# All five engines of the recurrence blocks 2 to 14 in one written order, with matmul banks read in place

## The chip, the cores and the metric

One core of one Trainium2 chip runs one launch of the kernel. The metric is the device time of that launch in microseconds (us). Differences are counted against the kernel before, whose three runs took 2610.59, 2611.43 and 2615.81 us (median 2611.43). Five engines work side by side, each through its own queue in order: TensorE (PE, matmuls), VectorE (DVE), ScalarE (ACT), GpSimd (POOL), and SyncE (SP), which here only issues DMAs.

## The reference, cut to what matters

One decoder layer over 2048 positions of width 1024. A normalised input goes through one large projection into two groups of heads, an SSD group and an RWKV7 group; both are mixed back, and a gated convolutional feed-forward follows. The part at issue is the RWKV7 group and the convolution that feeds the SSD group:

```python
p = p + (_token_shift(p) - p) * f32(mu)              # own column and the column one position before
r, w_lo, k, v, a_lo, g_lo = jnp.split(p, [i1, i2, i3, i4, i5], axis=-1)
...
def step(S, inp):                                    # the recurrence, one position after the other
    r_t, w_t, k_t, v_t, a_t, b_t = inp
    sa = jnp.einsum("bhij,bhj->bhi", S, a_t)
    S = S * w_t[:, :, None, :] + sa[..., None] * b_t[:, :, None, :] + v_t[..., None] * k_t[:, :, None, :]
    return S, jnp.einsum("bhij,bhj->bhi", S, r_t)
...
xbc = jax.nn.silu(_causal_dwconv(xbc, conv_w, conv_b))   # four taps: positions t-3 to t
```

All arithmetic is float32; the kernel computes its large products from float16 halves of weights and activations.

## The kernel before, in words

The first of three phases, `phase_R`, takes the sequence in 16 blocks of 128 positions. The weights stay in SBUF. For one block `it` it does, in the names of the code:

- `load`: reads 128 rows of x, normalises them, splits them into a high and a low float16 half, and turns both by a DMA transpose into `xt`. Three columns of the block before stand ahead of the 128, for the shift and the taps.
- `d`, groups 0 to 13: the projection, 24 matmuls of 128x129 each (line 301). Two groups share one PSUM bank of the tag `mm`, which has two buffers. After the second group ACT copies the bank to SBUF (`raw`, line 439) and writes the columns scaled by one minus mu (line 441); DVE adds the columns one position earlier, scaled by mu, out of `raw` (line 443). Groups 0 and 1 give `WA` and `GL`, then `tk`, `tr`, `tv` follow.
- `conv`, groups 0 to 7: the same with 131 columns and the same `mm` banks. ACT copies the bank (`rc`, line 455); POOL makes the first tap with the bias (line 464); DVE adds three taps for each of the two groups (line 469); ACT takes a tanh (line 473), DVE finishes the silu (line 474), SP stores.
- `low`, `scan`, `keys`, `norm`, `receptance`: decays, their running sums (`Pv`, a scan on DVE, line 508), their exponentials (`Pi` and `Pv`, ACT, lines 512 and 513), and the normalised keys. `norm` starts with the product `nq` and needs a logarithm and an exponential on ACT, each with a table load (lines 514 and 529).
- `gram`: the within-chunk products, masked by DVE into `G` (line 563). `solve` and `chain`: a triangular inverse, 31 pairs of small DVE operations (`tmp`, line 594, and `xl`, line 597), each of which needs the one before; its input goes out to HBM and back in another layout (`ATd`, `atl`), and so does its result (`XTd`, `XT`).
- `turn`, `merge`: DVE transposes a quarter of `XT` into `XW` (line 639), and two rounds of small products (`pw`, `po`) complete the inverse. `own`, `update`, `state`, twice, for the two chunks of 64 positions: the part of the recurrence that goes from chunk to chunk. `update` makes `pu`, which ACT copies to `UV` (line 696); `state` makes `pS` from it (line 713), and DVE adds it to the kept state `S`.
- `values`, `gate`, `finish`: the group norm, the bonus and the gate; the result is stored for the next phase.

The loop over blocks is a software pipeline. In iteration `it` the front part (`f`) works on block `it`, the back part (`b`) on block `it - 1`, the last piece (`a`) on block `it - 2`, and `n.load` prepares block `it + 1`. The table `PLAN`, a text of words such as `f.d.0 b.values`, gives the order in which iterations 2 to 14 call the functions. PE follows that order to the letter (its schedule is manual throughout). DVE and ACT follow the written order in iteration 0 alone; from iteration 1 on the tile framework's scheduler chooses, at build time, the order of DVE, ACT, POOL and SP. On the chip each engine then executes its fixed list, and an instruction that waits holds up all that stand behind it on its engine.

Within a function all instructions are issued at one place of `PLAN`. So the chain of block `it - 1` stands complete on DVE ahead of the scan of block `it`.

The later phases, the SSD group with the mixing (`phase_S`) and the feed-forward (`phase_F`), are not touched.

## Time and profile before

The profiled execution has a span of 2614.0 us from its first to its last instruction, with a mean granted PE clock of 0.975. That is 2.6 us over the median of the three runs and inside their range.

| stretch | length, us | PE busy | DVE busy | ACT busy | POOL busy | PE clock |
|---|---|---|---|---|---|---|
| whole program | 2614.0 | 2438.8 | 1968.8 | 1211.4 | 1310.1 | 0.975 |
| iterations 2 to 14, 145.0 to 865.5 us | 720.5 | 676.4 | 570.3 | 410.3 | 352.2 | 0.99 |
| one of the 13 iterations, mean | 55.42 | 52.03 | 43.87 | 31.56 | 27.10 | |

Iteration 2 begins near 145 us and iteration 15 near 865.5 us; both are read from the start of `f.d.0` on PE (the product `vt`, which `PLAN` puts behind the first three `d` groups, starts some 2.8 us later). Busy time of an engine is the union of its instructions. Matmuls overlap, so 24 matmuls of 222 ns each take 1.4 us together. In a row of the timeline the first number is the start, the second the length of the group, and the bracket gives the idle time of the engine ahead of it and the work that ended it.

### The profile page before, as it was taken

What the parts mean: (1) busy time and instruction counts of PE and PEld (TensorE: products, weight loads), DVE (VectorE), ACT (ScalarE), POOL (GpSimd) and SP (SyncE); (2) the same over time, 40 slices, a digit from 0 to 9 for tenths busy, and PEclk for the clock granted to TensorE, in tenths of its full rate; (3) what the DMA queues carried; (4) which work ended last, traced back from release to release, by engine and by line L of the source; (5) the groups of instructions that cost most, each with busy time, mean ns of one, the idle gap of its engine ahead of it and who ended that gap; (6) DMA issues with size and microseconds to landing.
All of it is one profiled execution on the core that took longest, in us unless ns stands there. A gap on an engine that the chain in (4) does not pass through costs nothing. (4 is left out here: it accounts for less than half of the span.)

```text
span 2614.0 us, 53918 instructions
## 1 busy us (share of the span) xinstructions
PE 2438.8 (93%) x21212; PEld 1535.9 (59%) x21212; DVE 1968.8 (75%) x3687; ACT 1211.4 (46%) x2467; POOL 1310.1 (50%) x1356
## 2 busy tenths in 40 slices
PE   5899999999999889999987999999989999999998
PEld 4788888888888755555543444444434444444443
DVE  7778777788877665677788889999999836455557
ACT  7455556555555444444544544544544433223132
POOL 2344444544545353445677675866858613213035
PEclk8999999999999989999998999999989999999999
DMA  7323222332232353556575534444435543333252
GB/s 219 73 69 68 54 58 61 68 83 55 57 62 61 80 177 96 172 144 188 146 216 177 173 133 165 138 173 173 149 126 197 166 145 101 102 99 106 85 159 107
DMA packets 344414, 319.14 MB, mean 122 GB/s; under 512 B 203232, under 2 KB 248672, under 8 KB 340832
## 3 DMA queue, kind: packets, MB, share of 16 engines
q1 hardware_dynamic: 342864, 314.12, 40.7%
q8 instruction: 166, 2.72, 0.4%
q10 hardware_dynamic: 1296, 1.58, 0.2%
q14 instruction: 88, 0.72, 0.1%
HBM read 187.85 MB, written 110.99 MB: 114 GB/s over the span
## 5 line engine op out<-in xcount | busy, mean ns | idle before, releaser
L1401 PE MATMUL u<-b,w 128*128 128x512 f16 x3696 | 812.6, 382 | 27.5 <-DVE C L1419 12.1
L1401 PEld LDWEIGHTS <-w 128*128 128x128 f16 x3696 | 363.6, 98 | 473.6 <-issue 39.8
L301 PE MATMUL d<-xt,wr 128*128 128x129 f16 x5376 | 342.1, 226 | 18.5 <-DMA xt<-xh 14.8
L301 PEld LDWEIGHTS <-wr 128*128 128x128 f16 x5376 | 327.2, 101 | 34.5 <-ACT wr L264 14.8
L1637 PE MATMUL d<-dw,fa 128*128 128x512 f16 x1512 | 333.7, 380 | 4.7 <-DVE dw L1601 2.3
L1637 PEld LDWEIGHTS <-fa 128*128 128x128 f16 x1596 | 156.9, 98 | 205.7 <-issue 19.3
L1419 DVE TENSOR_TENSOR C<-u,C 128x512 f32<-128x512 f32 x220 | 150.4, 684 | 156.7 <-PE u L1401 151.4
L301 PE MATMUL c<-xt,wc 128*128 128x131 f16 x3072 | 201.3, 224 | 26.3 <-ACT tr L441 17.3
L301 PEld LDWEIGHTS <-wc 128*128 128x128 f16 x3072 | 184.5, 99 | 42.6 <-issue 34.0
L1650 DVE TENSOR_TENSOR acc<-d,acc 128x512 f32<-128x512 f32 x212 | 140.0, 682 | 54.4 <-PE d L1637 53.5
L469 DVE SCALAR_TENSOR_TENSOR ca<-rc,cw,ca 128x128 f32<-128x128 f32 x384 | 130.7, 384 | 46.5 <-POOL ca L464 45.4
L1247 POOL TENSOR_TENSOR fa<-p,fa 128x512 f16<-128x512 f32 x100 | 142.3, 1437 | 40.0 <-ACT fa L1242 40.0
L1454 DVE SCALAR_TENSOR_TENSOR p<-C,fpar,p 128x1024 f32<-128x1024 f32 x88 | 129.4, 1470 | 35.4 <-ACT p L1450 35.2
L1249 DVE SCALAR_TENSOR_TENSOR w<-us,w 128x512 f16<-128x512 f32 x132 | 143.4, 1097 | 16.1 <-ACT w L1242 15.1
L597 DVE TENSOR_TENSOR xl<-xl,tmp 128x60 f32<-128x60 f32 (+24 forms) x465 | 140.7, 303 | 12.2
L594 DVE TENSOR_TENSOR tmp<-atl,xl 128x60 f32<-128x60 f32 (+24 forms) x465 | 121.7, 262 | 36.6 <-DMA atl<-ATd 24.7
L1454 DVE SCALAR_TENSOR_TENSOR a<-C,fpar,a 128x1024 f32<-128x1024 f32 x88 | 125.7, 1428 | 4.9 <-ACT a L1450 3.5
L1373 POOL TENSOR_TENSOR us<-us,us 128x512 f32<-128x512 f32 x66 | 106.7, 1619 | 41.5 <-DVE w L1249 21.5
L1242 ACT ACTIVATE fa<-p 128x512 f16<-128x512 f32 x110 | 65.6, 623 | 132.4 <-DVE p L1467 120.6
L1460 POOL COPY fcarry<-C 128x2 f32<-128x2 f32 x88 | 39.0, 444 | 165.0 <-DVE C L1419 165.0
L1415 ACT ACTIVATE C<-u 128x512 f32<-128x512 f32 x88 | 52.1, 593 | 145.6 <-PE u L1401 128.9
L1242 ACT ACTIVATE w<-us 128x512 f16<-128x512 f32 x132 | 80.6, 624 | 80.7 <-POOL us L1373 44.2
(316 smaller groups left out, 4534.3 us busy)
## 6 DMA issues: line engine op xcount, KB each, us to landing
UW<-w SPq DMA_DIRECT2D x154, 256.0 KB
w<-UW SPq DMA_DIRECT2D x154, 256.0 KB
us<-in_w_u_dram SPq DMA_DIRECT2D x88, 256.0 KB
DW<-dw SPq DMA_DIRECT2D x70, 256.0 KB
dw<-DW SPq DMA_DIRECT2D x56, 256.0 KB
hs<-HN SPq DMA_DIRECT2D x48, 256.0 KB
r<-in_w_d_dram SPq DMA_DIRECT2D x10, 1024.0 KB
xin<-in_x_dram SPq DMA_DIRECT2D x16, 512.0 KB
```

What stands on the lines that cost most here:

```text
L301: nc.tensor.matmul(ps, w[:, a, kt, :], xt[:, b, kt, cols], start=n == 0, stop=n == 3 * KT - 1)
L469: V.scalar_tensor_tensor(out=acc[:, q], in0=raw[:, q, k:k + 128], scalar=cw[:, g + q, k:k + 1], in1=acc[:, q], op0=ALU.mult, op1=ALU.add)
L594: chain.tensor_tensor(out=tmp[:, :m, :n], in0=atl[:, j, j + 1:32].unsqueeze(1).to_broadcast([P, m, n]), in1=xl[:, :m, j:j + 1].to_broadcas ...
L597: chain.tensor_tensor(out=xl[:, :m, j + 1:32], in0=xl[:, :m, j + 1:32], in1=tmp[:, :m, :n], op=ALU.add)
L1242: S.activation(h, src, AF.Copy, **({} if scale is None else {"scale": scale}))
L1247: {"V": V, "G": G_}[engine].tensor_tensor(out=l, in0=src, in1=h, op=ALU.subtract)
L1249: V.scalar_tensor_tensor(out=l, in0=src, scalar=scale, in1=h, op0=ALU.mult, op1=ALU.subtract)
L1401: nc.tensor.matmul(bk[at], self.w[i][:, u, k, :], self.half.b[i][:, k, v, :], start=start and n == 0, stop=n == 11, skip_group_check=True)
L1419: op("V", .61, lambda: V.tensor_tensor(out=part(j, x), in0=bk[at], in1=part(*a), op=ALU.add), (("u", 4 * s + at), (*(c0, c1)[a[0]], a[1])) ...
L1454: V.scalar_tensor_tensor(out=o[j], in0=C[j][:, 2 - d:1026 - d], scalar=cw[:, g, 2 - d:3 - d], in1=o[j], op0=ALU.mult, op1=ALU.add)
L1637: nc.tensor.matmul(bk[s, t], pairs[m].a[i][:, u, t * P:t * P + P], pairs[m].w[n][0][:, v, :], start=new and m == 0 and u == v == 0, stop=m ...
L1650: V.tensor_tensor(out=acc[j][:, t], in0=bk[s, t], in1=acc[j][:, t], op=ALU.add)
```

## The change

Three things change, all in `phase_R`, for blocks 2 to 14 (`direct` in the code).

1. Every function now returns a list of small steps, each one or a few instructions of one engine. `PLAN` is rewritten: a word such as `b.solve/30` issues step 30 of `solve` of block `it - 1`, and a word without a number issues the steps that are left. A function's steps can so stand at many places, and some stand in the next iteration: the chain has its steps 9 to 29 at the end of one iteration and 30 to 70 spread over the first half of the next. In iterations 2 to 14 the manual schedule holds for DVE, ACT, POOL and SP too. PE's products stand in another order as well.
2. The copies `raw` and `rc` are gone. DVE's shifted columns and its taps read the `mm` bank in PSUM itself.
3. The first tap with the bias is made by ACT out of PSUM instead of by POOL out of SBUF. The one-element logarithm of `scan` is gone.

Iterations 0, 1 and 15 and the drain keep the order of the functions that they had; ahead of iterations 2 and 15 whatever steps are left over are issued.

```diff
 PLAN = """
-f.d.0 f.d.1 b.values f.low.0 f.d.2 a.finish.1 f.d.3 f.d.4 f.low.1 f.scan f.d.5 f.d.6 f.d.7 b.own.0 f.d.8 f.conv.0
+b.solve/30 b.solve/31 b.d.13/1 b.solve/32 b.solve/33 f.d.0 f.d.1/0 f.d.1/1 a.finish.0/1 b.conv.5/10 b.solve/34
...
         class Block:
             def __init__(self, it):
-                self.it, self.sf = it, f"_{it}"
+                self.it, self.sf, self.direct = it, f"_{it}", 1 < it < iters - 1
+                self.todo, self.m = {}, {}
...
+            def do(self, name, *a, only=None):
+                key = (name, *a)
+                if key not in self.todo:
+                    self.todo[key] = getattr(self, name)(*a)
+                steps = self.todo[key]
+                for i in range(len(steps)) if only is None else (only,):
+                    step, steps[i] = steps[i], None
+                    if step:
+                        step()
...
             def d(self, g):
...
+                def past(u):
                     V.scalar_tensor_tensor(
-                        out=dst, in0=raw[:, q, 0:128], scalar=mus[:, g + q:g + q + 1], in1=dst, op0=ALU.mult, op1=ALU.add)
+                        out=dst(u), in0=m["d" if self.direct else "raw", e][:, u, 0:128], scalar=mus[:, e + u:e + u + 1], in1=dst(u), op0=ALU.mult,
+                        op1=ALU.add)
+                return [
+                    product, *(() if self.direct else (raw,)), lambda: own(0), lambda: own(1), lambda: past(0),
+                    lambda: past(1)]
...
+                if self.direct:
+                    m["rc", e] = m["c", e]
+                return [product, *(() if self.direct else (raw,)), *(self.taps(g) if post else ())]
...
+                    if self.direct:
+                        S.activation(
+                            m["ca", e][:, q], m["rc", e][:, q, 3:131], AF.Identity, scale=cw[:, e + q, 3:4],
+                            bias=cb[:, e + q:e + q + 1])
+                        return
                     G_.tensor_scalar(
...
-        hands = {getattr(mybir.EngineType, x) for x in ("DVE", "Activation")}
-        begun = ExitStack()
-        begun.enter_context(tc.manual_schedule(engines=hands))
+        hands = [{getattr(mybir.EngineType, x) for x in some} for some in (
+            ("DVE", "Activation"), ("DVE", "Activation", "Pool", "SP"))]
+        held = ExitStack()
+        held.enter_context(tc.manual_schedule(engines=hands[0]))
         for it in range(iters + 1):
-            if it == 1:
-                begun.close()
+            if it in (1, iters - 1):
+                held.close()
+            elif it == 2:
+                held.enter_context(tc.manual_schedule(engines=hands[1]))
...
-                go(blk, name, *a)
+                n = it + {"n": 1, "f": 0, "b": -1, "a": -2}[who]
+                if 0 <= n < iters:
+                    blocks[n].do(name, *(int(v) for v in a), only=int(part) if part else None)
```

What this moves is shown at three places, for block 8 and the iteration around it. In the rows a name before the arrow is written and those behind it are read; the number behind a name tells its copies apart.

**ACT around the exponentials of the scan (`Pi`).** Before:

```order
L441 ACTIVATE tk_8618<-d_4_8774,omu 128x128 x2
L512 ACTIVATE Pi_8626<-Pv_8624 128x8x64
L439 ACTIVATE raw_6_8910<-d_6_8861 128x258
L441 ACTIVATE tr_8619<-d_6_8861,omu 128x128 x2
L513 ACTIVATE Pv_8624<-Pv_8624 128x512
L514 ACT_TABLE_LOAD
```

Now:

```order
L532 ACTIVATE tr_8611<-d_6_8689,omu 128x128
L678 ACT_TABLE_LOAD
L678 ACTIVATE sq_8746<-nq_8783,tiny 128x512
L679 ACT_TABLE_LOAD
L679 ACTIVATE sq_8746<-sq_8746 128x512
L532 ACTIVATE tr_8611<-d_8_8751,omu 128x128
L648 ACTIVATE Pi_8504<-Pv_8805 128x8x64
L532 ACTIVATE tr_8611<-d_8_8751,omu 128x128
L650 ACTIVATE Pv_8805<-Pv_8805 128x512
L571 ACTIVATE ca_0_8905<-c_0_8852,cb,cw 128x128 x2
```

The copies out of the bank `d_6` stood behind `Pi`, which needs the scan; now they stand ahead of it and of `norm`'s two table loads, and there is no `raw`. The first taps `ca_0` are ACT's and stand behind `Pv`.

**ACT around the copy of the second `update` (`UV` from `pu`), near the end of the iteration.** Before:

```order
L686 ACTIVATE qs_9494<-pq_9473 64x512
L620 ACTIVATE BT_9496<-bt_8_9498 128x512
L473 ACTIVATE ct_6_9469<-ca_6_9460 128x256
L439 ACTIVATE raw_10_9553<-d_10_9504 128x258
L441 ACTIVATE tv_8625<-d_10_9504,omu 128x128 x2
L696 ACTIVATE UV_8684<-pu_9559 64x512
```

Now:

```order
L885 ACTIVATE qs_9275<-pq_9211 64x512
L587 ACTIVATE ct_4_9311<-ca_4_9135 128x256
L532 ACTIVATE tv_8612<-d_10_9286,omu 128x128
L901 ACTIVATE UV_8531<-pu_9277 64x512
L613 ACTIVATE GL_8462<-GL_8462 128x128
L532 ACTIVATE tv_8612<-d_10_9286,omu 128x128
L797 ACTIVATE BT_9425<-bt_8_9251 128x512
```

The tanh `ct_6` of the last convolution pair is no longer ahead of `UV` (it stands in the next iteration). On PE, `PLAN` had `b.update.1 f.d.12 b.state.1`; now three groups, `f.d.10`, `f.d.11` and `f.d.12`, stand between `b.update.1/0` and `b.state.1/2`.

**DVE from the end of the chain to `turn`.** Before:

```order
L597 TENSOR_TENSOR xl_8203<-xl_8203,tmp_8204 128x8
L508 SCALAR_TENSOR_TENSOR Pv_8624<-smask,thw_8622 128x512
L443 SCALAR_TENSOR_TENSOR tk_8618<-raw_4_8855,mus,tk_8618 128x128 x2
L443 SCALAR_TENSOR_TENSOR tr_8619<-raw_6_8910,mus,tr_8619 128x128 x2
L535 TENSOR_TENSOR tk_8618<-tk_8618,tm_9082 128x512
L639 STREAM_TRANSPOSE XW_9060<-XT_232 32x256 x2
```

Now:

```order
L759 TENSOR_TENSOR xl_8088<-xl_8088,tmp_8237 128x8
L535 SCALAR_TENSOR_TENSOR tr_8611<-d_6_8689,mus,tr_8611 128x128
L640 SCALAR_TENSOR_TENSOR Pv_8805<-smask,thw_8587 128x512
L680 SCALAR_TENSOR_TENSOR kkn_8715<-sq_8746,kkn_8715 128x512
L535 SCALAR_TENSOR_TENSOR tr_8611<-d_8_8751,mus,tr_8611 128x128 x2
L475 COPY xt_8847<-xt_7817 128x16x3
L684 SCALAR_TENSOR_TENSOR AR_8850<-kkn_8715,Pi_8504 128x4x128
L581 SCALAR_TENSOR_TENSOR ca_0_8905<-c_0_8852,cw,ca_0_8905 128x128 x6
L824 STREAM_TRANSPOSE XW_8968<-XT_232 32x256
L683 TENSOR_TENSOR tk_8610<-tk_8610,tm_8808 128x512
L824 STREAM_TRANSPOSE XW_8968<-XT_232 32x256
```

The scan, `norm`'s product with `kkn` and six taps of the first convolution pair now stand between the chain's last step and the two transposes; the taps read the bank `c_0`.

On PE, `merge.0`, which reads `XW`, stood directly behind `conv.1`; it now stands behind `conv.4`. On SP the two DMA transposes of `n.load` stood among the four stores of `ATd` and ahead of the four loads of `atl`; they now stand behind all eight. The last of the four loads of `XT` stands behind the stores of `conv.7`, of `xt` and of the finished block.

More of the change, by code (lines that the diff above doesn't have):

```diff
@@ L223 @@
+f.transposed.0/2 f.solve/27 f.d.11/4 b.state.1/6 b.finish.0/0 n.load/9 f.solve/28 f.solve/29 f.d.11/3 f.d.13/2
 """
@@ L554, in gram @@
             def gram(self, c):
+                m = self.m
                 side = c == 1 and 1 < self.it < iters - 1
[L556 to L561 removed]
@@ L562, in gram, with products @@
-                for hh in range(2):
+                def products():
+                    pg = m["gr", c] = [self.ms(f"gr{c}0"), bank("gr11" + self.sf, "B") if side else self.ms(f"gr{c}1")]
+                    for j in range(4):
+                        for hh in range(2):
+                            nc.tensor.matmul(
+                                pg[hh][:, j, :], self.BK[64 * hh:64 * hh + 64, j, c, :],
+                                self.AR[64 * hh:64 * hh + 64, j, c, :], start=True, stop=True)
@@ new lines, in back @@
+                def back(q):
+                    K.marks["atl"] = nc.sync.dma_start(
+                        self.atl[32 * q:32 * q + 32].rearrange("p i j -> p (i j)"),
+                        m["ATd"].rearrange("c b h i j -> (c b h) (i j)"))
+                return [
+                    *(lambda c=c, b=b: out(c, b) for c in range(2) for b in range(2)),
+                    *(lambda q=q: back(q) for q in range(4)),
+                    lambda: nc.sync.dma_start(
+                        self.xl.rearrange("p c i -> p (c i)"), K.cst_dram[:, COFF["x0"][0]:COFF["x0"][1]]),
+                    *(step for k in range(0 if begin else 8) for step in self.chain(k)),
+                ]
```

677 lines of the change are left out of this document (403 added, 274 removed).

## The prediction

> **What bounds the kernel now.** The change touches 13 iterations only, so I first cut these out of the span, in the view of busy time by stretches. Its columns are start and end, length, then busy time and instructions of PE, its weight loads, DVE, ACT and POOL, then the granted PE clock and the DMA share.
>
> ```profile
> 258.40:316.00 57.60, 54.35 (x851) 50.44 (x849) 44.15 (x132) 31.63 (x74) 28.17 (x33) 0.94 0.31 62
> ...
> 479.60:534.00 54.40, 51.30 (x853) 47.60 (x851) 43.72 (x131) 31.52 (x74) 27.13 (x32) 1.00 0.30 65
> ...
> 145.00:865.50 720.50, 676.42 (x11034) 627.22 (x11032) 570.28 (x1697) 410.34 (x964) 352.24 (x406) 0.99 0.29 63
> ```
>
> PE is busy for 676.4 of 720.5 us. The 44.1 us that it idles, 3.39 an iteration, are all that a better order can win while PE's work stays. DVE idles for 150.2 us, 11.56 an iteration, ACT and POOL for half the time: none of them bounds by its sum. At full clock an iteration holds 51.3 us of PE work; at 0.94 it holds 54.35.
>
> The next view is PE's waits over the same stretch (who waited, for whom, us in total, times, longest):
>
> ```profile
> PE c L301 <- ACT tr L441: 17.3, 11, 1.7
> PE pS L713 <- ACT UV L696: 17.2, 13, 2.2
> PE pw L650 <- DVE XW L639: 6.3, 13, 1.1
> PE gr L559 <- DVE BK L542: 2.7, 12, 0.2
> ```
>
> They add up to 43.5 of the 44.1 us, and they come back in every iteration. What is behind them shows in the timeline of one iteration, first PE, then ACT, then DVE and SP.
>
> ```profile
> 495.42 1.16 PE L682 MATMUL pq<-S,AR 128*128 128x128 f32 x8
> 496.41 1.54 PE L301 MATMUL d<-xt,wr 128*128 128x129 f16 x24
> 499.68 1.56 PE L301 MATMUL c<-xt,wc 128*128 128x131 f16 x24 [1.72 <-ACT tr L441]
> 501.08 1.54 PE L301 MATMUL d<-xt,wr 128*128 128x129 f16 x24
> ...
> 504.50 0.69 PE L650 MATMUL pw<-XW,G 32*32 32x32 f32 x30 [0.30 <-DVE XW L639]
> ...
> 526.03 1.14 PE L693 MATMUL pu<-qs,XT 64*64 64x64 f32 x16
> 527.11 1.55 PE L301 MATMUL d<-xt,wr 128*128 128x129 f16 x24
> 529.50 0.69 PE L713 MATMUL pS<-UV,BT 128*64 128x64 f32 x16 [0.84 <-ACT UV L696]
> ```
>
> ```profile
> 498.21 0.63 ACT L512 ACTIVATE Pi<-Pv 128x512 f32<-128x512 f32 x1 [5.17 <-DVE Pv L508]
> 498.75 0.37 ACT L439 ACTIVATE raw<-d 128x258 f32<-128x258 f32 x1
> ...
> 506.28 0.69 ACT L528 ACTIVATE sq<-nq,tiny 128x512 f32<-128x512 f32 x1 [0.29 <-PE nq L527]
> 506.98 1.28 ACT L529 ACT_TABLE_LOAD   x1
> 508.28 0.63 ACT L529 ACTIVATE sq<-sq 128x512 f32<-128x512 f32 x1
> ...
> 527.77 0.42 ACT L473 ACTIVATE ct<-ca 128x256 f32<-128x256 f32 x1 [2.22 <-DVE tmp L594]
> 528.10 0.37 ACT L439 ACTIVATE raw<-d 128x258 f32<-128x258 f32 x1
> 528.36 0.62 ACT L441 ACTIVATE tv<-d,omu 128x128 f32<-128x128 f32 x2
> 528.86 0.58 ACT L696 ACTIVATE UV<-pu 64x512 f32<-64x512 f32 x1
> ```
>
> ```profile
> 496.87 0.17 DVE L597 TENSOR_TENSOR xl<-xl,tmp 128x8 f32<-128x8 f32 x1
> 496.96 1.22 DVE L508 TENSOR_TENSOR_SCAN Pv<-smask,thw 128x512 f32<-128x512 bf16 x1
> ...
> 504.01 0.43 DVE L639 STREAM_TRANSPOSE XW<-XT 32x256 f32<-32x256 f32 x1 [0.37 <-DMA XT<-XTd]
> ...
> 516.19 1.28 DVE L563 TENSOR_TENSOR G<-gr,cst 128x512 f32<-128x512 f32 x2
> ...
> 526.58 0.19 DVE L594 TENSOR_TENSOR tmp<-atl,xl 128x31 f32<-128x31 f32 x1 [1.00 <-DMA atl<-ATd]
> ```
>
> All four waits are queues, not work. The convolution waits 1.72 us for a bank, since ACT's copies out of it stand behind `Pi`, which waits 5.17 us for the scan, which stands on DVE behind the last step of the chain. `pS` waits 0.84 us for `UV`, behind `raw`, `tv` and a tanh, and that tanh waited for taps that stand on DVE behind the first step of the chain, which waited for `atl` from HBM. `pw` waits for the transposes, which wait for `XT` from HBM.
>
> **The change part by part.** Work first.
>
> ```profile
> L439 ACT ACTIVATE raw<-d 128x258 f32<-128x258 f32 x84 | 32.8, 390 | 30.4 <-PE d L301 30.1
> L455 ACT ACTIVATE rc<-c 128x262 f32<-128x262 f32 x48 | 18.5, 386 | 14.0 <-PE c L301 13.7
> L441 ACT ACTIVATE tv<-d,omu 128x128 f32<-128x128 f32 x48 | 14.9, 365 | 0.0
> L464 POOL TENSOR_SCALAR ca<-rc,cw,cb 128x128 f32<-128x128 f32 x96 | 62.6, 661 | 13.8 <-ACT rc L455 12.6
> ```
>
> These groups cover 12 iterations. ACT loses 7 x 390 + 4 x 386 = 4.27 us an iteration, and gains 8 first taps, which I price like its other 128x128 reads of the bank, 8 x 365 = 2.92: 1.35 us less. POOL loses 8 x 661 = 5.29 us. PE's matmuls stay. Both savings are worth nothing by themselves, hidden under 51.3 us of PE work; without that cover they would be worth the 1.35 us of ACT at most, where ACT is waited for.
>
> DVE keeps its instructions, but 14 shifted columns and 24 taps an iteration read PSUM. No such form is in the trace, so I bound it by rows with one input in PSUM and rows with both in SBUF (shortest, median and longest ns):
>
> ```profile
> L469 DVE SCALAR_TENSOR_TENSOR ca<-rc,cw,ca x288: 334/346/770, 174.1 to 802.8; 128x128 f32<-128x128 f32 x144
> L474 DVE SCALAR_TENSOR_TENSOR ca<-ct,ca x48: 409/425/1496, 178.0 to 803.7; 128x256 f32<-128x256 f32 x48
> L718 DVE TENSOR_TENSOR S<-tS,pS x48: 411/420/425, 185.8 to 808.2; 64x256 f32<-64x256 f32 x48
> L563 DVE TENSOR_TENSOR G<-gr,cst x48: 677/681/685, 182.2 to 791.6; 128x512 f32<-128x512 f32 x48
> ```
>
> At 256 columns PSUM costs 420 against 425 ns, and neither PSUM row has a tail, while the SBUF rows reach two to three times their median. So a tap costs between 334 and, with the whole of the SBUF tail kept, 381 ns (the mean, 109.7 us over 288); I take 346. That is up to 0.8 us of DVE saved, which I count at nothing, because DVE idles 11.56 us anyway.
>
> [...]
>
> Now the order, by the four waits. PE slots are differences of the starts quoted: a group of 24 takes 1.40 us (499.68 to 501.08), `pq<-S` 0.99.
>
> *A, the `mm` banks.* The copies out of `d_6` no longer wait for the scan, so 17.3 us go. In their place a convolution bank is now held for two ACT reads and six taps instead of one copy, and `conv.4` needs the bank of `conv.0` and `conv.1`. Ahead of those taps DVE and ACT have, counted from the end of `nq`: logarithm 0.69, table load 1.28, exponential 0.63, then `kkn` and `AR` at 0.68 each and two shifted columns at 0.35 (the rows of 512 and of 128 columns), the copy of three columns at 0.2 (an estimate; the smallest DVE row quoted is 0.17), six taps 2.08: 6.9 us. A hand-over takes 0.03 (498.18 to 498.21) to 0.06 us (529.44 to 529.50); with four at 0.1 it is 7.3, and 8.6 if the first table load too begins only then. PE has `own`, `d.9` and four convolution groups meanwhile, 0.99 + 5 x 1.40 = 7.99 us. So `conv.4` is between in time and 0.6 us late. I take 0.4 an iteration, nearer to the far end, because POOL's pieces too (`thw` ahead of the scan, `tm`, `sq`) stand at new places of its queue. Behind the taps on DVE wait the transposes for `merge.0`, which is B.
>
> *B, `merge.0`.* From the chain's last step (497.04) to the last transpose (504.44) it took 7.4 us, 6.2 of them DMA to the first. The chain is now cut in two and its last three steps stand behind a shifted column of `d.7`; so it ends some 2 us behind `d.7` on PE, and `XT` lands at about 8.3. `merge.0` now has `d.8`, `nq`, `own`, `d.9` and five convolution groups ahead of it, 0.99 x 2 + 7 x 1.40 = 11.8 us. The DMA is hidden by 3.5 us, even with the stores that SP now issues between the four loads of `XT`, as only the first two feed `turn`. But the transposes stand behind the six taps, with a product of `tk` between them: 0.43 + 0.68 + 0.43 = 1.54 us behind the taps, against one group of 1.40 on PE. I charge 0.3, between nothing (taps early) and 0.8 (taps late as in A).
>
> *C, `pS`.* Three groups, 4.2 us, stand between `pu` and `pS`, instead of one. ACT's queue holds one read of `d.11` ahead of `UV`: 2.8 + 0.37 + 0.59 + 0.2 = 3.96 us. In time by 0.2; I charge 0.1. All taps now stand ahead of the chain's first step, so a late `atl` no longer holds a tanh. `atl` itself comes earlier: 9.1 us lay between the last `G` (517.47) and the chain, in which SP issued a transpose of 2.02 us between the `ATd` stores and one of 1.24 ahead of the loads.
>
> ```profile
> 517.33 2.02 SPq L411 DMA_TRANSPOSE xt<-xh  x1
> ...
> 520.55 1.24 SPq L412 DMA_TRANSPOSE xt<-xin  x1
> ```
>
> Both now stand behind, which delays `xt` for the next block; PE first reads that at the start of the next iteration. Of the chain, 41 of 62 steps move into the next iteration, where DVE has to finish them by `d.7`, the eighth group on PE.
>
> *D, the rest* (`gr`, and hand-overs of instructions that used to be queued differently): 0.2, as before (2.7 us in 13).
>
> Sum: 13 x (0.4 + 0.3 + 0.1 + 0.2) = 13 us of idle PE stay of 44.1, so 31 us go. Taken from the profiled span, 2614.0 - 31 = 2583.0; that execution lies 2.6 us over the median, so for the median 2611.4 - 31 = 2580.4. Bounds of the sum: nothing stays, 2567; all bounds at their far end (0.6 + 0.8 + 0.4 + 0.2 = 2.0 an iteration, 26 us), 2593.
>
> **The rivals.**
>
> *The banks become the wait.* Speaks for it: two buffers, and eight readers of each convolution bank instead of one copy. Against it: the sum at A comes out even. If POOL's `thw` or `tm` come late as well and A and B each cost 1.2 us, 2.4 with nothing else, 31 us stay: gain 13, 2598.
>
> *The clock.* The iteration at 258.4 ran at 0.94 and cost 3 us more PE work. If a denser PE brought half of them there, PE's mean would be (51.3 + 54.35) / 2 = 52.8 instead of 52.03, and 13 x 0.8 = 10 us would be given back: 2590. Against it: that iteration idled 3.25 us and the one at 1.00 3.10, so the clock does not follow the idle time.
>
> *DVE becomes the bound* (the other side). Its list is fixed, and it now waits in order for ACT (`WX`, `sq`), POOL (`thw`, `sq`), PE (`gr`, `pS`) and HBM (`atl`) once each an iteration, with all that is behind them held. It has 43.87 us of work; it idles 11.56 now. As long as its waits stay under 7.5 us PE's 51.3 us decide; at 11.6 the gain is gone; at 13 an iteration takes 56.9, 13 x 1.45 = 19 us slower: 2630. For it: the steps of the chain have tails like `L474`, and many waits in one list. Against it: the chain's steps are there to fill the waits, and my walk through A to C finds about 7 us of them.
>
> **How the numbers follow.** The forecast 0.60, the banks 0.17, the clock 0.07, DVE as the bound 0.16, half of it within 0.2% (5 us, about what a measurement of this kernel can tell from no change) and half slower. So faster 0.84, same 0.08, slower 0.08. Predicted time 2580. The range runs from 2567, where PE idles no more, to 2603, past the banks and the clock, which leaves out DVE's cases, 0.16, and a little below.
>
> **What would show it.** In the profile after: the waits `c` for `tr` and `pS` for `UV` gone, PE idle near 1 us an iteration, mostly ahead of `c` (for DVE's taps, A) and of `pw` (B); iterations of 52.3 us at full clock; taps at 346 ns with no tail; POOL 5 us less busy an iteration. Wrong would be PE idling over 2 us at any one place, or DVE busy with little idle while PE waits for it.

## The result and the profile after

The changed kernel took 2585.93 us in the median (2579.7 to 2592.31 in four runs), the kernel before 2612.32 (2610.59 to 2615.81 in four): a ratio of 0.9897, 95% interval 0.9875 to 0.9919. The forecast had been 2580. The profiled execution has a span of 2579.2 us, 34.8 less than before.

The view of busy time by stretches of the changed kernel, with the columns as before (start and end, length, busy time and instructions of PE, weight loads, DVE, ACT, POOL, then the granted PE clock and the DMA share). The first row is one usual iteration, the second the one long one, the third iterations 2 to 14:

```profile
461.68:513.73 52.05, 50.69 (x852) 47.30 (x850) 43.38 (x132) 31.37 (x70) 21.41 (x24) 1.00 0.33 68
618.77:677.28 58.51, 55.31 (x852) 51.55 (x849) 41.85 (x132) 31.46 (x70) 21.36 (x24) 0.91 0.28 61
145.97:833.10 687.13, 663.28 (x11010) 618.35 (x11007) 562.06 (x1690) 407.40 (x909) 280.46 (x301) 0.99 0.29 66
```

The 13 iterations take 687.1 us instead of 720.5, 33.4 less; everything else is as long as it was. PE idles 23.9 us (687.13 - 663.28) instead of 44.1. That is 20.2 of the 33.4; the other 13.1 are PE work that became shorter, of which no term of the prediction spoke. An iteration at full clock now holds 50.69 us of it (51.1 to 51.3 before), some 7 us in 13. The rest, about 6, is the clock: PE ran at half clock for 20.5 us in five of the 13 iterations before, for 10.2 us in one now.

PE's waits over the same 13 iterations (who waited, for whom, us in total, times, longest):

```profile
PE c L324 <- DVE ca L581: 13.9, 11, 1.3
PE po L844 <- DMA XT<-XTd: 4.4, 6, 1.8
PE c L324 <- ACT qs L885: 1.5, 1, 1.5
PE c L324 <- ACT ca L571: 1.3, 1, 1.3
```

All four waits of before are gone: `c` for `tr` as a wait of every iteration, `pS` for `UV`, `pw` for `XW`, `gr` for `BK`. In their place stand two. A convolution group waits for the six taps in every iteration, 1.26 us (three rows name it, by whatever came last), and `po`, the second round of the inverse's products, waits for a transfer of `XT` in six of them.

The timeline of one iteration of the changed kernel, by engine PE, DVE, POOL and SP (start, length, work; the bracket is the idle time ahead and who ended it; the one `po` is of another iteration):

```profile
487.93 1.56 PE L324 MATMUL c<-xt,wc 128*128 128x131 f16 x24 [1.26 <-DVE ca L581]
...
650.55 0.69 PE L844 MATMUL po<-XT,XW 32*32 32x32 f32 x32 [1.85 <-DMA XT<-XTd]
...
481.61 0.70 DVE L680 SCALAR_TENSOR_TENSOR kkn<-sq,kkn 128x512 f32<-128x512 f32 x1 [0.40 <-ACT sq L679]
...
483.00 0.35 DVE L535 SCALAR_TENSOR_TENSOR tr<-d,mus,tr 128x128 f32<-128x128 f32 x1 [0.44 <-ACT tr L532]
...
483.44 2.40 DVE L684 SCALAR_TENSOR_TENSOR AR<-kkn,Pi 128x512 f32<-128x512 f32 x1
485.77 2.01 DVE L581 SCALAR_TENSOR_TENSOR ca<-c,cw,ca 128x128 f32<-128x128 f32 x6
...
483.45 0.61 POOL L913 TENSOR_TENSOR tS<-S,Pi 64x256 f32<-64x256 f32 x1
484.03 1.26 POOL L687 TENSOR_TENSOR sq<-kkn,Pv 128x512 f32<-128x512 f32 x1
...
485.22 0.46 SPq L771 DMA_DIRECT2D XT<-XTd  x1
485.72 0.56 SPq L507 DMA_DIRECT2D XN<-xt  x1
486.39 1.56 SPq L1000 DMA_DIRECT2D YR<-yo  x1
488.33 0.49 SPq L771 DMA_DIRECT2D XT<-XTd  x1
```

`AR`, one product of 128x512 on DVE, takes 2.40 us. It starts 0.01 us ahead of POOL's `tS` and ends 0.55 us behind POOL's `sq`. The six taps behind it release the bank of `c`. On SP the last of the four loads of `XT` stands behind the store `YR`, whose issue takes 1.56 us.

By line (shortest, median and longest ns), the first row of the kernel before, the others of the changed one:

```profile
L538 DVE SCALAR_TENSOR_TENSOR AR<-kkn,Pi x13: 681/686/1790, 177.4 to 839.2; 128x512 f32<-128x512 f32 x13
```

```profile
L684 DVE SCALAR_TENSOR_TENSOR AR<-kkn,Pi x13: 2401/2404/2408, 169.8 to 803.1; 128x512 f32<-128x512 f32 x13
L581 DVE SCALAR_TENSOR_TENSOR ca<-c,cw,ca x312: 296/341/352, 172.2 to 825.1; 128x128 f32<-128x128 f32 x156
L571 ACT ACTIVATE ca<-c,cb,cw x104: 448/457/460, 169.8 to 821.4; 128x128 f32<-128x128 f32 x104
```

`AR` had 0.69 us in the median and now has 2.40 in all 13 iterations, not as a tail. The taps that read PSUM take 341 ns and have no tail. The first tap on ACT takes 457.

The long iteration, in short stretches of the same view:

```profile
648.00:652.00 4.00, 2.15 (x59) 1.96 (x57) 2.02 (x6) 1.86 (x5) 0.76 (x2) 1.00 0.29 72
652.00:662.00 10.00, 10.00 (x97) 9.23 (x95) 5.81 (x14) 4.54 (x8) 3.25 (x3) 0.51 0.24 57
```

The wait of `po` for 1.85 us ends at 650.55. From 652 the clock stands at half for some ten microseconds, and PE's work in this iteration is 4.6 us longer than usual (55.31 against 50.69). With these 4.6 us the wait of 1.85 us cost three and a half times its length.

### The profile page after: what moved, and what is told of

It is laid out like the page before. It is cut to its first block, busy times and chain, and to the rows that moved or that the text cites. A ratio compares the mean times of both kernels' runs of the same rounds, so it can differ in the third digit from the quotient of the medians.

```text
span 2579.2 us, 53771 instructions
## 1 busy us (share of the span) xinstructions
PE 2421.4 (94%) x21197; PEld 1528.3 (59%) x21212; DVE 1965.7 (76%) x3687; ACT 1209.7 (47%) x2415; POOL 1242.9 (48%) x1252
## 5 line engine op out<-in xcount | busy, mean ns | idle before, releaser
L1657 PEld LDWEIGHTS <-w 128*128 128x128 f16 x3696 | 363.2, 98 | 472.8 <-issue 36.9
L324 PE MATMUL d<-xt,wr 128*128 128x129 f16 x5376 | 336.2, 225 | 18.3 <-DMA xt<-xh 15.1
L324 PEld LDWEIGHTS <-wr 128*128 128x128 f16 x5376 | 322.0, 101 | 34.8 <-ACT wr L287 15.0
L324 PE MATMUL c<-xt,wc 128*128 128x131 f16 x3072 | 196.4, 225 | 25.3 <-DVE ca L581 13.9
L1505 DVE SCALAR_TENSOR_TENSOR w<-us,w 128x512 f16<-128x512 f32 x132 | 145.8, 1115 | 14.9 <-ACT w L1498 13.7
L759 DVE TENSOR_TENSOR xl<-xl,tmp 128x60 f32<-128x60 f32 (+24 forms) x465 | 117.7, 253 | 12.0
L753 DVE TENSOR_TENSOR tmp<-atl,xl 128x60 f32<-128x60 f32 (+24 forms) x465 | 100.3, 216 | 20.8 <-DMA atl<-ATd 3.2
L581 DVE SCALAR_TENSOR_TENSOR ca<-c,cw,ca 128x128 f32<-128x128 f32 x312 | 96.8, 340 | 14.3 <-ACT ca L571 12.0
```

Source lines behind the costliest of these rows:

```text
L324: nc.tensor.matmul(ps, w[:, a, kt, :], xt[:, b, kt, cols], start=n == 0, stop=n == 3 * KT - 1)
L753: chain.tensor_tensor(out=self.tmp[:, :k, :n], in0=self.atl[:, j, j + 1:32].unsqueeze(1).to_broadcast([P, k, n]), in1=self.xl[:, :k, j:j + ...
L759: chain.tensor_tensor(out=self.xl[:, :k, j + 1:32], in0=self.xl[:, :k, j + 1:32], in1=self.tmp[:, :k, :n], op=ALU.add)
L1505: V.scalar_tensor_tensor(out=l, in0=src, scalar=scale, in1=h, op0=ALU.mult, op1=ALU.subtract)
L1657: nc.tensor.matmul(bk[at], self.w[i][:, u, k, :], self.half.b[i][:, k, v, :], start=start and n == 0, stop=n == 11, skip_group_check=True)
```

## The experiments

One table for all of them: iterations 3 to 13, read from the start of `vt` in iteration 3 to that in iteration 14, in one profiled execution each; idle is the length less PE's busy time. The column on the right is the median time of the whole kernel; E7 and E8 have one time alone. The kernel before was timed again beside them, and each ratio in the text is against that time: 2618.0 us beside E1 to E4, 2616.4 beside E5 to E8, 2613.1 beside E9 to E11.

| kernel | 11 iterations, us | PE busy | PE idle | whole kernel, us |
|---|---|---|---|---|
| before | 605.6 | 569.9 | 35.7 | 2612.3 |
| changed | 581.3 | 562.5 | 18.7 | 2585.9 |
| E3 new order alone | 602.1 | 575.7 | 26.4 | 2614.9 |
| E4 in place, old order | 612.3 | 575.4 | 36.9 | 2622.2 |
| E5 new order, ACT's first tap, copies kept | 586.8 | 570.0 | 16.8 | 2590.6 |
| E2 copy of the convolution banks alone | 575.8 | 559.8 | 16.0 | 2592.0 |
| E1 `AR` behind the taps | 581.8 | 566.9 | 14.9 | 2585.4 |
| E7 `update` close to `state` | 592.6 | 564.3 | 28.3 | 2609.4 |
| E8 `Pi` ahead of the copies of `d_6` | 608.1 | 572.9 | 35.3 | 2619.0 |
| E9 `AR` early | 594.8 | 573.6 | 21.2 | 2606.0 |
| E10 `XT` early | 572.6 | 557.6 | 15.0 | 2576.5 |
| E6 both early | 561.4 | 557.6 | 3.8 | 2562.6 |
| E11 both early, copies kept | 580.4 | 563.7 | 16.8 | 2591.6 |

In these 11 iterations PE's work is 557.6 to 559.8 us where the clock never falls (E6, E10 and E2, with 1.00 in each iteration); in the kernels with the new order, what is above comes mostly from half clock (their mean granted clock there is 0.96 to 0.99). Since the mean granted clock of one kernel differs from run to run (0.971 to 0.978 in the 15 runs of the kernel before beside E9 to E11), the right column and the left ones need not agree to the microsecond.

### What the change consists of: E3, E4, E5

**E3: the new order alone.** Every bank is copied again and POOL makes the first tap.

```diff
+                    if self.direct and ("raw", e) not in m:
+                        raw()
...
-                        out=dst(u), in0=m["d" if self.direct else "raw", e][:, u, 0:128], ...
+                        out=dst(u), in0=m["raw", e][:, u, 0:128], ...
...
-                    m["rc", e] = m["c", e]
+                    m["copy", e] = raw
...
-                    if self.direct:
-                        S.activation(
-                            m["ca", e][:, q], m["rc", e][:, q, 3:131], AF.Identity, ...)
-                        return
+                    if self.direct and q == 0:
+                        m["copy", e]()
                     G_.tensor_scalar(
```

> The written order alone: the copies raw and rc are back (each issued on ACT with the first read of its bank), the shifted columns and taps read SBUF, and POOL makes the first tap again. Theory (the four waits were queues, and the order alone takes them away): PE no longer waits for tr at the convolution, for UV at pS or for XW at pw, and at least 20 of the 26 us remain: 2580 to 2592 us. Rival (the reads in place bring the gain): the copies and POOL's 5.3 us bring the waits back, and the time is 2600 us or more.

Measured: 2614.9 us, ratio 0.9989, interval 0.997 to 1.0008. The theory that the order carries the gain falls. PE's waits, and the timeline of DVE and POOL around the first taps:

```profile
PE pw L839 <- DVE XW L823: 31.6, 26, 2.0
```

```profile
499.06 2.30 DVE L580 SCALAR_TENSOR_TENSOR ca<-rc,cw,ca 128x128 f32<-128x128 f32 x6 [2.44 <-POOL ca L574]
...
493.93 2.86 POOL L671 TENSOR_SCALAR tm<-tha,ka,kam 128x128 f32<-128x128 f32 x4 [1.19 <-DVE Pv L639]
...
497.33 1.26 POOL L686 TENSOR_TENSOR sq<-kkn,Pv 128x512 f32<-128x512 f32 x1
498.59 0.87 POOL L574 TENSOR_SCALAR ca<-rc,cw,cb 128x128 f32<-128x128 f32 x2
```

In the new order POOL's first tap stands behind `tm`, `tS` and `sq`; DVE waits 2.44 us for it, and PE waits for the transposes behind the taps, 31.6 us in all. The old waits are indeed gone, and this one replaces them. It is not all of the loss: of the 20.8 us by which E3's 11 iterations exceed the changed kernel's, 13.2 are PE's own work, at half clock for 3.41 us in most of them.

**E4: the old order, with banks read in place and the first tap on ACT.** In the kernel before, for blocks 2 to 14:

```diff
-                raw = wk.tile([P, 2, 129], F32, ...)
-                S.activation(raw, self.ps[:, :, 0:129], AF.Copy)
+                raw = self.ps
...
+                    if 1 < i < iters - 1:
+                        S.activation(acc[:, q], raw[:, q, 3:131], AF.Identity, scale=cw[...], bias=cb[...])
+                        continue
```

> The kernel before with the reads in place alone: in blocks 2 to 14 no raw and rc, DVE reads the banks, ACT makes the first tap; PLAN and the scheduler's order as before. Theory (the order brings the gain): the copies out of bank d_6 still stand behind the scan, and now DVE's two reads of that bank do too, so the convolution waits 1.7 us or more, pS waits as before; no gain, 2605 to 2640 us. Rival: 1.35 us less on ACT and 5.3 us less on POOL shorten the queues that PE waits for; 10 us or more faster than before.

Measured: 2622.2 us, ratio 1.0012, interval 0.9996 to 1.0029. PE's waits:

```profile
PE d L301 <- DVE tk L445: 23.4, 12, 2.0
PE d L301 <- DVE ca L477: 12.4, 12, 1.8
```

A bank read in place is held until DVE has come to it, and in the old order DVE comes late. This is the rival of the banks, at its full price, in the order in which it holds.

**E5: E3, with the first tap on ACT** out of the copy, so that it differs from the changed kernel in the copies alone.

```diff
-                    if self.direct and q == 0:
-                        m["copy", e]()
+                    if self.direct:
+                        if q == 0:
+                            m["copy", e]()
+                        S.activation(
+                            m["ca", e][:, q], m["rc", e][:, q, 3:131], AF.Identity, ...)
+                        return
```

> The written order with all copies of the banks back (raw and rc on ACT, DVE reads SBUF) but the first tap on ACT as in the changed kernel. The order with the copies and POOL's first tap had kept no gain (0.9989); in its trace the six taps waited 2.4 us for POOL's first tap, behind tm, tS and sq, and pw then waited for the transposes behind the taps. Theory (the first tap's engine decides): with ACT's first tap that wait is gone and most of the gain is back: 2585 to 2597 us, ratio 0.989 to 0.994. [...]

Measured: 2590.6 us, ratio 0.9898, interval 0.9884 to 0.9911, the changed kernel's own within the intervals. So the order needs ACT's first tap, and with that the gain is there; the reading in place adds nothing that this measurement can tell. PE's wait is at another place:

```profile
PE pw L844 <- DVE XW L828: 15.9, 22, 0.8
```

### Why the convolution waits: E2, E1

**E2: only the convolution banks are copied**, by ACT, ahead of the first tap; the shifted columns still read PSUM.

```diff
-                    m["rc", e] = m["c", e]
+                    m["copy", e] = raw
...
+                        if q == 0:
+                            m["copy", e]()
```

> The changed kernel with the convolution banks copied to SBUF by ACT again (one copy of 0.39 us ahead of the first tap); the order of everything else, the shifted columns out of PSUM and the first tap on ACT stay. Theory (the bank is held by the late taps): conv.4 needs only ACT's copy, so its wait of 1.26 us is gone and 10 to 15 us go; the taps read two SBUF operands again and get a tail beyond 500 ns, and ACT is 1.5 us busier an iteration, which may cost some of it elsewhere: 2570 to 2580 us. Rival (ACT is the tight one): the added copies hold up the reads behind them on ACT, new waits for ACT of 1 us or more an iteration appear, and it is slower than the changed kernel by 5 us or more.

Measured: 2592.0 us, ratio 0.9889, interval 0.9853 to 0.9924. The wait at `c` is gone, but the time is not the 2570 to 2580 us of the theory, and the new waits for ACT of the rival did not come either. `pw` waits for DVE instead:

```profile
PE pw L842 <- DVE XW L826: 14.3, 26, 0.8
```

The bank was the place where DVE's lateness showed, not its cause: with the bank free at once, the transposes behind the same six taps are what comes late.

**E1: `AR` behind the taps** on DVE.

```diff
-n.load/0 b.solve/72 f.norm/9 f.conv.0 ...
+n.load/0 b.solve/72 f.conv.0 ...
...
-f.conv.3/1 f.conv.3/2 b.turn/0 ...
+f.norm/9 f.conv.3/1 f.conv.3/2 b.turn/0 ...
```

> The changed kernel with one word of PLAN moved: the product AR<-kkn,Pi on DVE now stands behind the six taps of the first convolution pair instead of ahead of them. Theory (SBUF contention): the 1.26 us that conv.4 waits for the taps come from that product, which takes 2.40 us in all 13 iterations instead of 0.68 because it reads two SBUF operands while POOL runs tS and sq; behind the taps it meets an idle POOL. The wait falls from 1.26 to 0.2 us or less, 13 to 16 us less in all, 2565 to 2573 us, ratio about 0.984 to before. Rival (the bank itself): six taps and two ACT reads of one bank are too long whatever stands ahead of them; the wait stays at 1.0 us or more and the time within 4 us of the changed kernel.

Measured: 2585.4 us, ratio 0.9882, interval 0.985 to 0.9914. `AR` by line, then PE's waits (146 to 780 us):

```profile
L684 DVE SCALAR_TENSOR_TENSOR AR<-kkn,Pi x13: 678/678/681, 174.3 to 807.7; 128x512 f32<-128x512 f32 x13
```

```profile
PE po L844 <- DMA XT<-XTd: 6.6, 8, 2.7
PE pw L840 <- DVE XW L824: 3.7, 12, 0.3
PE c L324 <- DVE ca L581: 2.7, 11, 0.3
```

Away from `tS` and `sq` the same instruction takes 678 ns, and `c` waits 0.25 us instead of 1.26. So `AR`'s place beside these two cost it 1.7 us; the 14 us that were to follow from another place did not come. `po` and `pw`, which the wait at `c` had covered, now wait themselves, so that PE idles only 3.8 us less in the 11 iterations (14.9 against 18.7), and PE's work is 4.4 us longer there (566.9 against 562.5).

### Undoing one step each: E7, E8

**E7: `b.update.1/0` one step later** on PE, behind `f.d.11/0` instead of ahead of `f.d.10`, so that less work lies between `pu` and `pS`.

```diff
-b.gate/0 f.solve/10 b.own.1/2 b.update.1/0 f.d.10 f.conv.5/9 f.solve/11 n.load/7 f.d.11/0 ...
+b.gate/0 f.solve/10 b.own.1/2 f.d.10 f.conv.5/9 f.solve/11 n.load/7 f.d.11/0 b.update.1/0 ...
```

> The changed kernel with the second update moved behind d.11, so that one group instead of three stands between pu and pS on PE, as in the kernel before. Theory (ACT's queue): UV now has nothing late ahead of it on ACT, so pS waits 0.1 us or less an iteration. Rival (the distance on PE): pS waits 0.7 to 2.2 us for UV in each iteration as in the kernel before.

Measured: 2609.4 us in one run. `pS` does not wait here either, but `d.10`, now earlier, waits for the taps of `conv.4` and `conv.5` to leave its bank:

```profile
PE d L324 <- DVE ca L581: 8.7, 11, 0.8
```

So it was ACT's queue, not the distance on PE, that made `pS` wait in the kernel before. The time itself is 23 us above the changed kernel's. In iterations 3 to 13 PE idles 9.6 us more, the wait at `d` above all; iteration 14, with a mean granted clock of 0.90, takes 7.7 us more; the rest of this one run was not followed.

**E8: the scan and `Pi` ahead of the copies out of `d_6`**, on ACT and DVE, as they stood before.

```diff
-f.d.7/0 a.finish.1/7 ... f.low.1/7 f.d.8 f.d.7/2 b.solve/60 ...
+f.d.7/0 a.finish.1/7 ... f.low.1/7 f.d.8 b.solve/60 ...
...
-a.state.1/4 f.norm/2 ... f.scan/1 a.finish.1/8 f.norm/4
+a.state.1/4 ... f.scan/1 f.scan/3 f.d.7/2 f.d.7/1 f.d.7/4 f.d.7/3 f.norm/1 f.norm/2 a.finish.1/8 f.norm/4
```

> The changed kernel with the old queue at the scan: on DVE the scan stands ahead of the two reads of bank d_6, and on ACT Pi stands ahead of the copies out of it and norm's two steps behind. Theory (that queue made the wait of 1.7 us): the first convolution group waits 1 to 2.5 us for tr again in each iteration, and it is 5 to 25 us slower than the changed kernel. Rival (the wait went away because the chain is spread over two iterations, so the scan is early): the first convolution group waits 0.3 us or less.

Measured: 2619.0 us in one run. The wait of before is back, larger and twice an iteration, and the loss is more than the 5 to 25 us expected:

```profile
PE c L324 <- DVE tr L535: 44.5, 26, 3.2
```

### Both waits taken away: E6, E9, E10, E11

**E6: `AR` ahead of the last shifted column of `d.9` on DVE, and the four `XT` loads together on SP**, ahead of the stores `XN` and `YR`; the store `XC` of `conv.7` moves ahead of the chain's output.

```diff
-... b.own.0/1 b.solve/71 f.scan/1 ...
+... b.own.0/1 b.conv.7/11 b.solve/71 f.scan/1 ...
-... f.scan/3 f.d.9/4 f.d.9/1 f.d.9/3
+... f.scan/3 f.d.9/4 f.norm/9 f.d.9/1 f.d.9/3
-n.load/0 b.solve/72 f.norm/9 f.conv.0 b.solve/75 f.scan/4 f.norm/10 b.solve/76 f.conv.1/0 ...
+n.load/0 b.solve/72 f.conv.0 b.solve/75 f.scan/4 f.norm/10 b.solve/76 b.solve/77 b.solve/78 f.conv.1/0 ...
-... f.conv.1/6 b.conv.7/11 f.conv.3/0 f.conv.1/8 b.solve/78 f.conv.1/7
+... f.conv.1/6 f.conv.3/0 f.conv.1/8 f.conv.1/7
-... f.norm/12 b.solve/77 b.merge.0/1
+... f.norm/12 b.merge.0/1
```

> The changed kernel with two edits: AR<-kkn,Pi on DVE stands between the two shifted columns of d.9, ahead of POOL's tS and sq instead of beside them; on SP the store of conv.7 stands ahead of the chain's output and the four loads of XT follow one another, ahead of the stores of xt and of the finished block. With AR behind the taps the wait at conv.4 had fallen from 1.26 to 0.25 us, but pw waited 0.3 us for the transposes and po 0.4 us and more for the fourth load of XT, and an iteration still took 52.07 us. Theory (three waits one behind the other): with all three causes taken away an iteration takes 51.0 to 51.3 us at full clock, 10 to 13 us less in all than the changed kernel: 2568 to 2578 us, ratio 0.983 to 0.986. Rival (a loop over the engines of 52.05 us that moves its wait elsewhere): an iteration stays at 52.0 us or more, the wait under another name.

Measured: 2562.64 us (2559.89 to 2567.68 in five runs), ratio 0.9796, interval 0.9781 to 0.9812: it beats both kernels and the 2568 to 2578 us that were expected. Eleven iterations, then all that PE waits for in 200 to 780 us:

```profile
203.14:764.49 561.35, 557.60 (x9331) 520.25 (x9329) 456.82 (x1431) 344.51 (x770) 241.02 (x253) 1.00 0.30 69
```

```profile
PE c L324 <- DVE ca L581: 2.8, 11, 0.3
```

An iteration takes 51.03 us, of which PE idles 0.34, and the granted clock is 1.00 in the eleven.

**E9 and E10: the two halves of E6 alone.**

> AR stands ahead of the last shifted column of d.9's pair on DVE, as in the run that moved AR and the XT loads together, but SP's order is the changed kernel's. If the two places are separate waits that hide each other, the wait at c falls from 1.3 to 0.3 us an iteration and the wait of po for the fourth XT load grows from 0.4 to about 1.4 us, because that load hangs behind the store of the finished block and does not move: iteration 52.0 us, about 2585 us, nothing gained. If AR alone was the cost, the iteration is 51.1 us and the time about 2565 us.

> The loads of XT stand early on SP as in the run that moved both; AR stands where the changed kernel has it. If the waits are separate, po no longer waits (0.4 us an iteration in the changed kernel), c still waits 1.3 us: the iteration falls by at most 0.4 us, about 2580 to 2585 us. If the loads alone were the cost, the time is about 2565 us.

E9, `AR` alone, took 2606.0 us, ratio 0.9968, interval 0.9952 to 0.9984: some 20 us slower than the changed kernel, where no loss was expected. E10, the loads alone, took 2576.5, ratio 0.9852, interval 0.9825 to 0.988. PE's waits of E9 in 200 to 780 us:

```profile
PE po L844 <- DMA XT<-XTd: 17.3, 11, 2.8
PE c L324 <- DVE ca L581: 2.8, 11, 0.3
```

As the theory of two waits had it, what `c` lost `po` gained: 17.3 us in 11 iterations. PE's idle time is nearly the changed kernel's (21.2 against 18.7). What neither theory had is the other 11 us, PE's work of 573.6 against 562.5. One wait of E9 in the timeline, and the stretches around it:

```profile
335.69 0.81 PE L844 MATMUL po<-XT,XW 32*32 32x32 f32 x32 [2.57 <-DMA XT<-XTd]
```

```profile
332.00:336.00 4.00, 1.43 (x41) 1.28 (x39) 2.43 (x7) 1.56 (x4) 0.75 (x2) 1.00 0.57 139
336.00:348.00 12.00, 12.00 (x128) 11.14 (x123) 5.72 (x14) 5.25 (x9) 3.15 (x3) 0.50 0.22 51
```

Right behind the wait, from 336.10 by the record of the granted clock, PE runs at half clock for 13.65 us. The same happens, for 10.24 us each, behind the waits that end at 446.88, 505.05 and 826.25 us (1.36, 2.47 and 2.50 long), and not behind the other eight of 0.8 us or more, though one of them is the longest, 2.77. E9's mean granted clock was 0.966 to 0.971 in all its ten runs, E6's 0.977 to 0.980 in its five; the two differ in the order of SP's loads and stores alone. So the half clock came with the waits of `po`, and that is where most of E9's 20 us went: 11 are the longer work of these 11 iterations, and 5.4 more are iteration 14, where the fourth of the waits lies. E10 shows the other side: its iterations are 52.05 us with `c` waiting 1.26 us in each, none of the eleven falls to half clock, and by the medians it wins 9.5 us, though the two intervals just overlap. In the changed kernel's profile `po` had waited 4.4 us in all, and the half clock behind one of these waits had cost 4.6.

**E11: E6 with the copies of E5.**

> AR and the XT loads early as in the run that moved both, and the copies raw and rc back on ACT, so that DVE and the first taps (still ACT's) read SBUF. If reading in place is worth nothing, the time is that of the run that moved both, 2560 to 2568 us. If the copies hold the banks or ACT's queue longer once nothing else waits, PE waits for XW at pw (0.8 us an iteration in the run with the copies at the changed kernel's order) and the time is about 2573 us.

Measured: 2591.6 us, ratio 0.9918, interval 0.9892 to 0.9944, 29 us slower than E6 and some 19 more than expected. The wait is at `pw`, 16.8 us in 200 to 780. The six taps in the timeline, E11 with POOL's `sq`, then E6 with its own:

```profile
330.10 3.40 DVE L585 SCALAR_TENSOR_TENSOR ca<-rc,cw,ca 128x128 f32<-128x128 f32 x6 [0.62 <-ACT ca L575]
...
330.39 1.26 POOL L691 TENSOR_TENSOR sq<-kkn,Pv 128x512 f32<-128x512 f32 x1
```

```profile
478.59 2.03 DVE L581 SCALAR_TENSOR_TENSOR ca<-c,cw,ca 128x128 f32<-128x128 f32 x6 [1.21 <-ACT ca L571]
...
478.30 1.27 POOL L687 TENSOR_TENSOR sq<-kkn,Pv 128x512 f32<-128x512 f32 x1
```

The same six instructions, beside the same instruction of POOL, take 3.40 us with both inputs in SBUF and 2.03 with one in PSUM. Counted from the end of `nq` on PE, the taps start 6.06 us later in E11 and 6.31 in E6, so ACT's copies do not hold them up; they end 9.46 and 8.34 us later. Here reading in place is worth much: not for the copy that ACT saves, but since beside POOL's `sq` the six taps took 2.03 us out of PSUM and 3.40 out of SBUF.

E11 also shows, in part, behind which waits the half clock came. In each of its iterations 3 to 14 PE waits for the two transposes 0.70 and then 0.82 us. Here are two of these pairs, and the stretches around them:

```profile
280.45 0.24 PE L844 MATMUL pw<-XW,G 32*32 32x32 f32 x2 [0.70 <-DVE XW L828]
281.52 0.69 PE L844 MATMUL pw<-XW,G 32*32 32x32 f32 x30 [0.82 <-DVE XW L828]
...
334.01 0.24 PE L844 MATMUL pw<-XW,G 32*32 32x32 f32 x2 [0.70 <-DVE XW L828]
335.08 0.69 PE L844 MATMUL pw<-XW,G 32*32 32x32 f32 x30 [0.82 <-DVE XW L828]
```

```profile
279.06:282.47 3.41, 1.88 (x50) 1.55 (x48) 3.31 (x7) 1.87 (x5) 1.27 (x1) 1.00 0.60 143
282.47:285.88 3.41, 3.41 (x56) 3.15 (x55) 3.13 (x9) 1.82 (x5) 1.16 (x3) 0.50 0.05 17
333.67:337.09 3.42, 2.25 (x56) 2.10 (x56) 3.39 (x7) 1.86 (x5) 1.32 (x1) 1.00 0.56 139
337.09:340.50 3.41, 3.41 (x76) 3.07 (x75) 3.34 (x10) 2.20 (x6) 1.12 (x2) 1.00 0.23 57
```

In the records of the granted clock of the kernel before and of the changed kernel every stretch between two changes is a whole multiple of 3.41 us long, and in E3, E6, E9, E10 and E11 the stretches at half clock between 146 and 838 us have one, three or four times that length, so that the clock of these executions can be cut into steps of 3.41 us. Six of the twelve pairs lie inside one such step (one of them but for 0.03 us), as the first one shown, and the next step runs at half clock. In the other six a step ends inside or between the two waits, at 333.67 us in the second one shown, and the clock stays full. E9 fits but for one wait: its four waits with half clock had 2.57, 1.36, 1.69 and 2.04 us in the step just ahead of it, and seven of the others at most 1.30 us in any step. The longest was cut into 1.75 and 1.02 us; why the 1.75 did not bring the half clock is not known.

## Why the prediction was right, and where it was not

The time, 2586 against 2580, lies inside the range, and so does its direction. The way to it was only partly the one foretold.

**The four waits go.** Right, and E8 shows the first of them by its undoing: with the exponentials ahead of the copies of `d_6` again, 44.5 us of waiting are back. That the order alone does it was wrong, though. I took the move of the first tap to ACT as worth nothing by itself, "hidden under 51.3 us of PE work". E3 and E5 differ in that tap alone, and by 24 us: in the written order POOL's taps stand behind three other pieces of POOL's work, and DVE's taps and transposes wait for them. The step that failed is the cover: it was named for POOL's sum, not for the place in POOL's queue at which the tap now stood.

**A, the `mm` banks.** The place, the releaser and the direction were right, the size was not: 0.4 us an iteration was taken, with bounds of 0 and 0.6, and 1.26 was measured. The term that was mis-sized is `AR` "at 0.68": it took 2.40, since it had come to stand beside POOL's `tS` and `sq`. I had priced it by the row of another product of 512 columns, `G` (L563, 681 ns), which reads one input from PSUM. `AR`'s own row of before, 686 in the median, has 1790 as its longest, and that was the warning. Counted from the end of `nq` (478.43), the taps end at 487.78, 9.35 us instead of 7.3, of which `AR` makes 1.72. E1 takes the cause away and 1.0 of the 1.26 goes. This is also the price that the rival of the banks had put on A (1.2), with another cause: not `thw` or `tm` late, but two engines in each other's way.

**B, `merge.0`.** 0.3 was taken, none was measured: PE's wait at A comes ahead of `pw` and covers it. E1 and E2, which shorten that wait, bring `pw`'s out (0.31 us at a time in E1, 14.3 us over 13 iterations, so 1.1 each, in E2). The sentence that failed is that the stores between the `XT` loads do no harm "as only the first two feed `turn`". That is true of `turn`; the second round, `po`, reads what the fourth load brings, and it waited in six iterations, 4.4 us, one of which cost 4.6 more by the clock.

**C, `pS`, and D.** 0.3 together were taken, none was measured. In the iteration around 508 us of the changed kernel `UV` is ready 0.43 us ahead of `pS` (508.84 against 509.27), where 0.2 had been worked out.

**The reads out of PSUM.** 346 ns were taken for a tap and 341 measured, without a tail, as foretold. The copies to SBUF do not pay: E11 has them and is 29 us slower than E6. Counted "at nothing, because DVE idles 11.56 us anyway" holds for the changed kernel (E5 is as fast) and no longer once the other waits are gone. ACT's first tap was mis-sized, 457 ns for 365; nothing waited for the difference.

**The sum.** 13 us of idle PE were to stay, 23.9 did: A alone makes 16.7 of them (13.9 + 1.5 + 1.3). Against that the profiled execution has 13.1 us less of PE work, which I had held constant. So the 31 us of the forecast and the 34.8 measured there agree by two errors of opposite sign. By the medians the gain is 26.4.

**The rivals.** DVE is not the bound: it idles 125 us in the 13 iterations (687.13 - 562.06). The clock had a chance of 0.07 and a wrong cause: not a denser PE, since E6, the densest, has a clock of 1.00 in iterations 3 to 13, but waits of PE (E9). My ground against it, that two iterations of before idle alike at different clocks, compared sums over an iteration where single waits decide.

What stays open: why the longest of E9's waits does not bring the half clock, why the half clock lasts 3.41 us behind some waits and 10 to 14 behind others, and why PE's work at full clock is about 0.5 us an iteration shorter in the new order. No run was made for any of these.

## What to carry to other kernels

When instructions are put in another order, look for each on the path at what the other engines run in the same microsecond, and price it at least at the longest duration that its row shows, not at its median (here 1.79 us against 0.69; it came to 2.40). When a wait is taken away, name the wait that it had covered and take that away in the same edit: here one of two edits alone brought 9.5 us, the other cost 20, and both together brought 23. A short wait of PE can cost several times its length (1.85 us of it came to 6.45 with the half clock behind it in the changed kernel), so the profile is to be read for the clock just behind it.

## What the runs showed of the hardware

**DVE and POOL in each other's way.** A DVE product of 128x512 with both inputs in SBUF took 0.68 us behind the six taps (E1) and 2.40 beside two POOL products with both inputs in SBUF (0.61 and 1.26 us, in the changed kernel); six taps took 3.40 us beside `sq` with both inputs in SBUF (E11) and 2.03 with one in PSUM (E6), where they had taken 2.01 in the changed kernel with no work of POOL beside them. Who pays differs: beside POOL's four `tm`, which have a tensor input in SBUF and scalars, `AR` kept its 0.68 us in E6, and the four took 2.59 us there instead of 2.17 in the changed kernel. In the kernel before `AR` started 0.02 to 0.04 us behind `sq` in all 13 iterations: in eight it took 0.68 or 0.69 us and `sq` 1.84 or 1.85, in five 1.78 or 1.79 and `sq` 1.27.

**Half clock behind short waits.** Behind single waits of 1.36 to 2.57 us PE ran at half clock for 10.2 to 13.7 us; in E9 this followed four waits of twelve. Behind E11's pairs of 0.70 and 0.82 us it ran so for 3.41 us, where both lay in one step of the clock.
